# Two matmuls on the same weights become one of 512 columns, and the halves are added on the way out

## The chip, the cores and the metric

One NeuronCore of a Trainium2 chip runs the whole program. The metric is the device time of one execution in microseconds (us), taken as the median of three runs. TensorE (PE) multiplies into PSUM, an accumulator of eight banks of 512 float32 columns on each of 128 partitions. VectorE (DVE) and ScalarE (ACT) read PSUM and write SBUF. GpSimd (POOL) and SyncE (SP, which issues the weight loads) play a small part here.

## The reference, cut to what matters

Two layers work on a stream `h` of 256 tokens by 1024, float32. Each layer is a half step of SwiGLU, a mixer, and a second half step of SwiGLU; a last norm follows.

```
h = h + 1/2 * SwiGLU_a(RMSNorm(h))        # (silu(x @ w_gate) * (x @ w_up)) @ w_down, D_FF = 2816
u = RMSNorm(h);  z = u @ W_in             # columns: latents of MLA, diff q k v, pooling input p, gates
m = sum_i sigmoid(z_gate_i) * (y_i @ W_branch[i])
h = h + m @ W_out
h = h + 1/2 * SwiGLU_b(RMSNorm(h))
```

## The kernel before, in words

Every float32 operand of a product is split into two parts of 12 bits, `hi` and `lo`, so that three products of parts stand for one exact one: hi·hi, hi·lo and lo·hi. `mm3` (L162 to L165) issues these three matmuls into the same PSUM columns. Each matmul instruction is preceded by a load of its stationary operand, also when the operand is the same as before.

Two kinds of product exist. In `gemm_tokens` (L167) the stream is stationary and 512 (or 416) weight columns move. In `ffn` (gate and up products, L281 to L291) and in `gemm_dims` (L463 to L473; the columns C_P, C_DQ and C_DK of `W_in`) the weights are stationary: for each tile of 128 weight columns and each of the 8 tiles `k` of the contraction, `mm3` moves the 256 tokens of `u.xh(k)` and `u.xl(k)`. That is 4 half steps x 11 chunks x 2 weights x 2 tiles x 8 = 1408 calls in `ffn`, and 2 layers x 3 x 4 tiles x 8 = 192 in `gemm_dims`, 1600 triplets of 256 columns in all.

PSUM is used through three pools: four banks `acc`, three banks `tr` and one bank `o`. A chunk of `ffn` is 256 columns of gate and of up. In all chunks but the first, the two tiles of a weight share one bank, so a chunk takes two of the four `acc` banks. In the first chunk each tile has a bank of its own, two `acc` and two `tr`, of which half is used. `times` (L299) multiplies PSUM by the tokens' factors `rb` on the way out: one DVE instruction of 512 columns for each weight (L304), or four of 256 in the first chunk (L302). Then come SiLU on ACT (L307), the product of gate and up (L309) and its split into `ghi` and `glo` (L258, L259). `gemm_dims` puts two tiles into each bank, two banks for a call, and `scaled` (L475) takes each tile out with one DVE instruction (L478).

Each weight tile is loaded by one DMA on SP's queue, cast by ACT (`hi`, L158) and subtracted by DVE (`lo`, L159). There are three buffers each for the raw tile, `hi` and `lo`. `Norm` (L191) makes the stream's two parts: `hi` and `lo` are two tiles of [128, 8, 256], written half by half.

In the mixer `gemm_tokens` first makes the latents (C_CQ), whose two `acc` banks stay in use while squares, factors and copies are worked out (L429 to L447). Then follow C_P, C_DQ, the products of the latents (`mla_w_uq`, `ukv`), the attention, C_DK and C_DV. The order of instructions on each engine is not the order of the source: a planner in the framework sets it when the kernel is built, by program order and by what is ready and free. Each engine then runs its own list in order.

Of the kernel before, what the change touches and what calls it, by code (L numbers as in the profile page):

```python
# [11 lines left out]
F32 = mybir.dt.float32  # L12
F32R = mybir.dt.float32r
# [19 lines left out]
# columns of w_in  # L33
C_CQ, C_DQ, C_DK, C_DV, C_P, C_G = 0, 416, 928, 1440, 1952, 2464

# columns of the packed small parameters, per layer
# [8 lines left out]
def plan():  # L45
    """Weight tiles in the order of their use: (array, layer, first row tile, row tiles, first column, columns)."""
# [39 lines left out]
def trunk(ctx, tc, x, xt, positions, wall, small, lamrow, fnorm, out):  # L86
# [51 lines left out]
    # the input's loads, which go between those of the first weights  # L138
# [27 lines left out]

    def gemm_tokens(specs, xh, xl, n, before=None, tail=1):  # L167
        """Products with tokens on the partitions: one bank for each half of the tokens.

        The first half of the tokens is done ahead of the second in the last tiles, tail of them."""  # L170
# [15 lines left out]
    def rsqrt_mean(dst, src, n):  # L186
        """dst = (src / n + eps) ** -0.5"""
        nc.vector.tensor_scalar(out=dst, in0=src, scalar1=1.0 / n, scalar2=EPS, op0=ALU.mult, op1=ALU.add)
        nc.gpsimd.tensor_tensor(out=dst, in0=dst, in1=mhalf[:, :dst.shape[1]], op=ALU.pow)

    class Norm:  # L191
        """The transposed, scaled stream in two parts, and each token's factor, half by half."""

        def __init__(self, l, at):
            self.l, self.at = l, at
            self.hi = big([P, KD, S], F32R, "uhi")
            self.lo = big([P, KD, S], F32R, "ulo")
            self.ss = sp.tile([P, 2, 2], F32, tag="ss", name="ss", bufs=2)

        def half(self, n):  # L200
            for j in range(2):
# [7 lines left out]
                for i in range(2):  # L209
# [3 lines left out]
                    nc.scalar.activation(out=self.hi[:, k, :], in_=src, func=AF.Identity, scale=g)  # L213
                    nc.vector.scalar_tensor_tensor(
                        out=self.lo[:, k, :], in0=src, scalar=g, in1=self.hi[:, k, :].bitcast(F32),
# [3 lines left out]
        def first(self, k):  # L219
            """A tile of the same from the input, which comes in both layouts."""  # L220
            g = col(self.l, self.at + k)
            nc.sync.dma_start(out=xT[:, k, :], in_=xt[k * P:(k + 1) * P])
            nc.vector.tensor_scalar(out=self.hi[:, k, :], in0=xT[:, k, :], scalar1=g, scalar2=None, op0=ALU.mult)
            nc.vector.scalar_tensor_tensor(out=self.lo[:, k, :], in0=xT[:, k, :], scalar=g,
                                           in1=self.hi[:, k, :].bitcast(F32), op0=ALU.mult, op1=ALU.subtract)
# [12 lines left out]
        def row(self):  # L238
            """The factors along the free dimension, on every partition."""
# [9 lines left out]
        def xh(self, k):  # L249
            return self.hi[:, k, :]  # L250

        def xl(self, k):
            return self.lo[:, k, :]

    def split_evac(hi, lo, src, scale=None):
        """PSUM or SBUF -> the two parts, times a constant or a column."""
# [8 lines left out]
    def ffn(l, pre, u, following, midway=None):  # L265
        ghi = [big([P, 8, S], F32R, "ghi") for _ in range(3)]
        glo = [big2([P, 8, S], F32R, "glo") for _ in range(3)]
        for c in range(0, DFF, S):
            if c == 1024 and midway:
                midway(g[:, 0, :2])  # L270
            # transposed products, weights stationary: two tiles of each
            opened = bool(opening)
            w = [wsplit((f"{pre}_w_{n}", l, 0, KD, c, S)) for n in ("gate", "up")]
            if c == 0:
                # a bank for each tile, so that the first half of the stream serves them all
                ps = [[b()[:, :S] for _ in range(2)] for b in (acc, trp)]
                halves = [range(0, 4), range(4, 8)]
                order = [(n, i, k) for ks in halves for n in range(2) for i in range(2) for k in ks]
                if opened:
                    order = [(n, i, k) for n in range(2) for k in range(KD) for i in range(2)]  # L280
            else:  # L281
                banks = [acc() for _ in range(2)]
                ps = [[b[:, i * S:(i + 1) * S] for i in range(2)] for b in banks]
                order = [(n, i, k) for n in range(2) for i in range(2) for k in range(KD)]
            for n, i, k in order:
                wh, wl = w[n]
                ms = slice(i * P, (i + 1) * P)
                mm3(ps[n][i], wh[:, k, ms], wl[:, k, ms], u.xh(k), u.xl(k), k == 0, k == KD - 1)
# [10 lines left out]
            def times(dst, n):  # L299
                if c == 0:  # L300
                    for i in range(2):
                        nc.vector.tensor_tensor(out=dst[:, i, :], in0=ps[n][i], in1=rb, op=ALU.mult)  # L302
                else:
                    nc.vector.tensor_tensor(out=dst, in0=banks[n].rearrange("p (i s) -> p i s", i=2), in1=rbb, op=ALU.mult)  # L304
# [31 lines left out]
    # groups of heads in one bank of scores, every other head, on the same rows: (query tile, heads, keys)  # L336
# [3 lines left out]
    def tables(after):  # L340
        pi = sp.tile([P, 2], I32, tag="pi", name="pi", bufs=1)
        pr = tp.tile([P, S], I32, tag="C", name="pr")
        # the loads wait until the stream is under way
# [4 lines left out]
        # distances, exact where float32 holds them  # L348
# [22 lines left out]
        # rotary angles, reduced to [-pi, pi]  # L371
# [23 lines left out]
        # the learned lambda of each layer, and the head norm's gain times 1 - lambda_init  # L395
# [13 lines left out]
    def rope(eng, dst1, dst2, x1, x2, cos, sin, shape, out_shape=None):  # L409
        """The rotation of [x1 | x2]."""  # L410
# [9 lines left out]
    def mixing(l, u, following):  # L420
        wi = lambda c, n: [("w_in", l, k, 4, c, n) for k in (0, 4)]
        # -- latents and the shared rotary key
# [33 lines left out]
        # -- pooling input and differential q, k, transposed; v  # L456
# [6 lines left out]
        def gemm_dims(c, evac):  # L463
            w = [wsplit(spec) for spec in wi(c, 512)]
            for j in range(2):
                ps = acc()
                for i in range(2):
                    m = j * 2 + i
                    for k in range(KD):
                        wh, wl = w[k // 4]  # L470
# [379 lines left out]
```

## Time and profile before

| what | value |
|---|---|
| median of three runs (lowest, highest) | 1235.31 us (1235.24, 1237.77) |
| span of the profiled execution, first to last instruction | 1231.7 us |
| time outside that span, against the median | 3.6 us |
| mean granted clock of TensorE, of full speed | 0.999 |
| HBM traffic over the span | 172 GB/s |

The profile is of one execution. Its page gives the span and not that execution's own time from end to end. Busy times overlap (a matmul's record contains its run through the array), so the distance from one start to the next, not the recorded duration, is what a matmul costs in a stream.

### The profile page before, as it was taken

How to read it: one execution, taken by the hardware profiler on the slowest of the kernel's cores; microseconds unless marked ns; L12 is line 12 of the kernel's file. 1: busy time of each engine (PE TensorE's matmuls, PEld its weight loads, DVE VectorE, ACT ScalarE, POOL GpSimd, SP SyncE). 2: the span in 40 equal slices, each digit the busy share in tenths (PEclk: the TensorE clock that was granted, in tenths of full speed). 3: DMA queues.
4: the chain of work that ended last, by engine and by line, in shares of the span. 5: the costliest groups of instructions: out<-in, count | busy, mean ns of one | idle time of the engine just before them, and what ended most of it. 6: DMA issues, size and time to landing. Idle time of an engine off the chain costs nothing.

```text
span 1231.7 us, 19142 instructions
## 1 busy us (share of the span) xinstructions
PE 1216.1 (99%) x7912; PEld 1108.6 (90%) x7912; DVE 792.4 (64%) x1281; ACT 576.9 (47%) x891; POOL 69.3 (6%) x126
## 2 busy tenths in 40 slices
PE   7999999999999999999999999999999999999997
PEld 7999989998788899998899998899978888999986
DVE  6776655777757666664576664568686485766653
ACT  5454444446544554443454443455455444544442
POOL 0000000700100000000000000024010000000000
PEclk9999999999999999999999999999999999999999
DMA  8655455325345545554555555544343554455551
GB/s 276 239 184 181 175 181 191 120 93 189 137 171 176 192 172 179 181 191 168 187 199 176 191 182 188 175 146 145 110 165 135 177 202 171 171 188 188 189 171 68
DMA packets 34631, 213.13 MB, mean 173 GB/s; under 512 B 4080, under 2 KB 5488, under 8 KB 10992
## 3 DMA queue, kind: packets, MB, share of 16 engines
q1 hardware_dynamic: 33408, 210.52, 48.3%
q10 hardware_dynamic: 1136, 1.40, 0.4%
q8 instruction: 62, 1.02, 0.3%
q14 instruction: 25, 0.20, 0.1%
HBM read 210.85 MB, written 1.05 MB: 172 GB/s over the span
## 4 chain that ended last, share of the span: by engine, by line
PE 94%; DVE 3%; issue 2%; ACT 0%; DMA 0%; SPq 0%; POOLq 0%; POOL 0%
PE acc L163 28%; PE acc L164 28%; PE acc L165 28%; PE o L589 2%; PE tr L555 2%; PE tr L582 1%; PE tr L546 1%; PE tr L206 1%; DVE lo L159 1%; PE tr L163 1%; PE tr L165 1%; PE tr L164 1%; DMA xT<-xt 0%; PE tr L602 0%; PE acc L658 0%
## 5 line engine op out<-in xcount | busy, mean ns | idle before, releaser
L158 ACT CAST hi<-raw 128x1024 fp32r<-128x1024 f32 (+2 forms) x416 | 403.6, 1005 | 512.4 <-issue 326.3
L159 DVE TENSOR_TENSOR lo<-raw,hi 128x1024 fp32r<-128x1024 f32 (+2 forms) x416 | 481.4, 1173 | 223.1 <-ACT hi L158 222.2
L163 PE MATMUL acc<-uhi,hi 128*128 128x256 f32 x1536 | 439.2, 286 | 5.6 <-ACT hi L158 5.6
L165 PE MATMUL acc<-uhi,lo 128*128 128x256 f32 x1536 | 437.7, 285 | 1.5 <-DVE lo L159 1.5
L164 PE MATMUL acc<-ulo,hi 128*128 128x256 f32 x1536 | 437.7, 285 | 0.0
L163 PEld LDWEIGHTS acc<-uhi,hi 128*128 128x128 f32 x1536 | 296.7, 193 | 5.8 <-ACT hi L158 5.6
L165 PEld LDWEIGHTS acc<-uhi,lo 128*128 128x128 f32 x1536 | 296.6, 193 | 2.3 <-DVE lo L159 2.1
L164 PEld LDWEIGHTS acc<-ulo,hi 128*128 128x128 f32 x1536 | 296.8, 193 | 0.3
L164 PE MATMUL acc<-lo,ghi 128*128 128x512 f32 x352 | 137.4, 390 | 0.0
L165 PE MATMUL acc<-hi,glo 128*128 128x512 f32 x352 | 137.3, 390 | 0.0
L163 PE MATMUL acc<-hi,ghi 128*128 128x512 f32 x352 | 137.2, 390 | 0.0
L164 PE MATMUL acc<-lo,uhi 128*128 128x512 f32 (+1 forms) x256 | 99.6, 389 | 0.0
L163 PE MATMUL acc<-hi,uhi 128*128 128x512 f32 (+1 forms) x256 | 99.4, 390 | 0.0
L165 PE MATMUL acc<-hi,ulo 128*128 128x512 f32 (+1 forms) x256 | 98.8, 386 | 0.0
L163 PEld LDWEIGHTS acc<-hi,ghi 128*128 128x128 f32 x352 | 66.1, 188 | 13.5
L165 PEld LDWEIGHTS acc<-hi,glo 128*128 128x128 f32 x352 | 66.1, 188 | 13.5
L164 PEld LDWEIGHTS acc<-lo,ghi 128*128 128x128 f32 x352 | 66.1, 188 | 13.5
L304 DVE TENSOR_TENSOR g<-acc,rb 128x512 f32<-128x512 f32 x40 | 27.7, 693 | 78.5 <-PE acc L165 78.5
L574 ACT ACTIVATE e<-e,mx 128x128 f32<-128x128 f32 (+1 forms) x96 | 42.8, 446 | 57.4 <-DVE mx L570 35.4
L304 DVE TENSOR_TENSOR sg<-acc,rb 128x512 f32<-128x512 f32 x40 | 27.7, 692 | 49.6 <-PE acc L165 49.6
L164 PEld LDWEIGHTS acc<-lo,uhi 128*128 128x128 f32 x256 | 48.1, 188 | 9.7 <-issue 1.3
L163 PEld LDWEIGHTS acc<-hi,uhi 128*128 128x128 f32 x256 | 48.0, 188 | 9.3 <-issue 0.7
(199 smaller groups left out, 1222.4 us busy)
## 6 DMA issues: line engine op xcount, KB each, us to landing
raw<-wall SPq DMA_DIRECT2D x184, 1024.0 KB, 4.8
raw<-wall SPq DMA_DIRECT2D x10, 512.0 KB, 3.5
raw<-wall SPq DMA_DIRECT2D x18, 256.0 KB, 5.4
raw<-wall SPq DMA_DIRECT2D x4, 832.0 KB, 4.4
raw<-wall SPq DMA_DIRECT2D x2, 768.0 KB, 4.1
xT<-xt SPq DMA_DIRECT2D x8, 128.0 KB, 4.6
h<-x SPq DMA_DIRECT2D x4, 256.0 KB, 5.8
fn<-fnorm ACTq DMA_DIRECT2D x1, 512.0 KB, 3.8
```

Source lines behind the costliest of these rows:

```text
L158: nc.scalar.copy(out=hif[:, ks], in_=rawf[:, ks])
L159: nc.vector.tensor_tensor(out=lof[:, ks], in0=rawf[:, ks], in1=hif[:, ks].bitcast(F32), op=ALU.subtract)
L163: nc.tensor.matmul(ps, lhsT=lh, rhs=rh, start=start, stop=False)
L164: nc.tensor.matmul(ps, lhsT=lh, rhs=rl, start=False, stop=False)
L165: nc.tensor.matmul(ps, lhsT=ll, rhs=rh, start=False, stop=stop)
L206: nc.tensor.transpose(out=ps[:, (i * 2 + t) * P:(i * 2 + t + 1) * P], in_=h[:, t, k * P:(k + 1) * P], identity=ident)
L304: nc.vector.tensor_tensor(out=dst, in0=banks[n].rearrange("p (i s) -> p i s", i=2), in1=rbb, op=ALU.mult)
L546: nc.tensor.matmul(ps[:, i * nk:(i + 1) * nk], lhsT=qT[:, hd, qt * P:(qt + 1) * P], rhs=kT[:, hd, :nk], start=True, stop=True)
L555: nc.tensor.matmul(ps[:, i * nk:(i + 1) * nk], lhsT=dqT[a:a + 32, hd // 2, qt * P:(qt + 1) * P], rhs=dkT[a:a + 32, hd // 2, :nk], start=Tr ...
L574: nc.scalar.activation(out=e[:, sl], in_=e[:, sl], func=AF.Exp, bias=mx[:, i:i + 1], scale=-(2.0 ** -(hd + 1)) if slope else -1.0, accum_o ...
L582: nc.tensor.transpose(out=ptr[:, j * P:(j + 1) * P], in_=e[:, j * P:(j + 1) * P], identity=ident)
L589: nc.tensor.matmul(o[:, hd * 64:(hd + 1) * 64], lhsT=eT[:, j * P:(j + 1) * P], rhs=v[:, kt, hd * 64:(hd + 1) * 64], start=(kt == 0), stop= ...
```

## The change

A new `mm_wide` replaces `mm3` where weights are stationary. The stream's two parts lie side by side in new tiles `u` of [128, 4, 2, 256], one for each half of the contraction. A first matmul with `wh` moves both parts, 512 columns, into a whole bank; a second with `wl` moves the 256 columns of `xh` onto the bank's first half. `joined` puts the halves together: ACT copies the second half to SBUF, and DVE adds the first half to it. Each tile of 128 weight columns now has a bank of its own: a chunk of `ffn` takes four `acc` banks (two `acc` and two `tr` in the first chunk, as before), and a call of `gemm_dims` four. The multiplication by `rb` follows from SBUF, 512 columns at a time, or by the former instruction of `scaled`. In `gemm_dims` the intermediate sum lies in a buffer `both` of tag C, of which there are two. `gemm_tokens` is as before. The rest of the diff takes comments away.

```diff
+    def mm_wide(ps, wh, wl, u, k):
+        nc.tensor.matmul(ps, lhsT=wh, rhs=u.both(k), start=k == 0, stop=False)
+        nc.tensor.matmul(ps[:, :S], lhsT=wl, rhs=u.xh(k), start=False, stop=k == KD - 1)
+    def joined(dst, ps):
+        nc.scalar.copy(out=dst, in_=ps[:, S:])
+        nc.vector.tensor_tensor(out=dst, in0=ps[:, :S], in1=dst, op=ALU.add)
...
-            self.hi = big([P, KD, S], F32R, "uhi")
-            self.lo = big([P, KD, S], F32R, "ulo")
+            self.u = [big([P, 4, 2, S], F32R, "u") for _ in range(2)]
...
-            return self.hi[:, k, :]
+            return self.u[k // 4][:, k % 4, 0, :]
...
-            return self.lo[:, k, :]
+            return self.u[k // 4][:, k % 4, 1, :]
+        def both(self, k):
+            return self.u[k // 4][:, k % 4].rearrange("p e s -> p (e s)")
...
-            if c == 0:
-                ps = [[b()[:, :S] for _ in range(2)] for b in (acc, trp)]
...
-            else:
-                banks = [acc() for _ in range(2)]
-                ps = [[b[:, i * S:(i + 1) * S] for i in range(2)] for b in banks]
+            ps = [[b() for _ in range(2)] for b in (acc, trp if c == 0 else acc)]
...
-                mm3(ps[n][i], wh[:, k, ms], wl[:, k, ms], u.xh(k), u.xl(k), k == 0, k == KD - 1)
+                mm_wide(ps[n][i], wh[:, k, ms], wl[:, k, ms], u, k)
...
-                if c == 0:
-                    for i in range(2):
-                        nc.vector.tensor_tensor(out=dst[:, i, :], in0=ps[n][i], in1=rb, op=ALU.mult)
-                else:
-                    nc.vector.tensor_tensor(out=dst, in0=banks[n].rearrange("p (i s) -> p i s", i=2), in1=rbb, op=ALU.mult)
+                for i in range(2):
+                    joined(dst[:, i, :], ps[n][i])
+                nc.vector.tensor_tensor(out=dst, in0=dst, in1=rbb, op=ALU.mult)
...
-            for j in range(2):
+            for m in range(4):
                 ps = acc()
-                for i in range(2):
-                    m = j * 2 + i
-                    for k in range(KD):
-                        wh, wl = w[k // 4]
-                        mm3(ps[:, i * S:(i + 1) * S], wh[:, k % 4, m * P:(m + 1) * P], wl[:, k % 4, m * P:(m + 1) * P],
-                            u.xh(k), u.xl(k), k == 0, k == KD - 1)
-                evac(j, ps.rearrange("p (i s) -> p i s", i=2))
+                for k in range(KD):
+                    wh, wl = w[k // 4]
+                    mm_wide(ps, wh[:, k % 4, m * P:(m + 1) * P], wl[:, k % 4, m * P:(m + 1) * P], u, k)
+                evac(m, ps)
...
-            def evac(j, ps):
-                for i in range(2):
-                    nc.vector.scalar_tensor_tensor(out=dst[:, j * 2 + i, :], in0=ps[:, i, :], scalar=const_(j * 2 + i), in1=rb,
-                                                   op0=ALU.mult, op1=ALU.mult)
+            def evac(m, ps):
+                both = tp.tile([P, S], F32, tag="C", name="both")
+                joined(both, ps)
+                nc.vector.scalar_tensor_tensor(out=dst[:, m, :], in0=both, scalar=const_(m), in1=rb,
+                                               op0=ALU.mult, op1=ALU.mult)
```

## Rows read from the trace of the kernel before

**Rows 1.** The page's first part: busy time of an engine, share of the span, instructions. PE and DVE.

```profile
PE 1216.1 (99%) x7912; PEld 1108.6 (90%) x7912; DVE 792.4 (64%) x1281; ACT 576.9 (47%) x891; POOL 69.3 (6%) x126
```

**Rows 2.** The waits of PE over the whole span: what waited for what, us in total, times, longest in us. These are all of them.

```profile
PE acc L163 <- ACT hi L158: 5.6, 1, 5.6
PE acc L165 <- DVE lo L159: 1.5, 2, 1.0
PE acc L163 <- DVE k L527: 1.0, 2, 0.5
PE o L589 <- DVE eT L584: 0.5, 2, 0.2
PE acc L163 <- DVE qr L518: 0.2, 1, 0.2
```

**Rows 3.** Instructions of one form, grouped by line (count | busy us, mean ns of one | idle before). The first product of a triplet with weights stationary, in `acc` and in `tr` banks.

```profile
L163 PE MATMUL acc<-uhi,hi 128*128 128x256 f32 x1536 | 439.2, 286 | 5.6 <-ACT hi L158 5.6
...
L163 PE MATMUL tr<-uhi,hi 128*128 128x256 f32 x64 | 18.4, 287 | 0.0
```

**Rows 4.** The timeline of PE: start us, duration us, line, operation. First and last of stretches without a gap: 25 matmuls of 256 columns in a chunk (24 distances), 19 of 512 columns in the down product (18 distances), 27 of 416 columns (26 distances), 12 of 256 columns on weights of 64 columns (11 distances).

```profile
80.11 0.28 PE L165 MATMUL acc<-uhi,lo 128*128 128x256 f32 x1
...
82.99 0.28 PE L165 MATMUL acc<-uhi,lo 128*128 128x256 f32 x1
...
149.81 0.39 PE L163 MATMUL acc<-hi,ghi 128*128 128x512 f32 x1
...
153.89 0.39 PE L163 MATMUL acc<-hi,ghi 128*128 128x512 f32 x1
...
204.82 0.36 PE L163 MATMUL acc<-hi,uhi 128*128 128x416 f32 x1
...
209.71 0.35 PE L165 MATMUL acc<-hi,ulo 128*128 128x416 f32 x1
...
238.42 0.27 PE L163 MATMUL acc<-cTh,hi 128*64 128x256 f32 x1
...
239.67 0.28 PE L165 MATMUL acc<-cTh,lo 128*64 128x256 f32 x1
```

**Rows 5.** The same view in the opening: 21 matmuls of 256 columns (20 distances), before the distances fall to those of rows 4 at 16.7 us.

```profile
12.06 0.42 PE L164 MATMUL acc<-ulo,hi 128*128 128x256 f32 x1
...
16.33 0.40 PE L163 MATMUL acc<-uhi,hi 128*128 128x256 f32 x1
```

**Rows 6.** Instructions of one form on DVE and ACT, whole span (count | busy us, mean ns of one | idle before): a DVE product of a PSUM operand and an SBUF operand at 256 and at 512 columns, a DVE product of two SBUF operands at 512, and an ACT instruction from PSUM at 256.

```profile
L302 DVE TENSOR_TENSOR sg<-acc,rb 128x256 f32<-128x256 f32 x8 | 3.0, 416 | 0.0
...
L304 DVE TENSOR_TENSOR sg<-acc,rb 128x512 f32<-128x512 f32 x40 | 27.7, 692 | 49.6 <-PE acc L165 49.6
...
L309 DVE TENSOR_TENSOR g<-g,sg 128x512 f32<-128x512 f32 x44 | 30.4, 692 | 1.9 <-ACT sg L307 0.5
...
L517 ACT ACTIVATE qn<-acc 128x256 f32<-128x256 f32 x8 | 2.9, 384 | 2.4 <-PE acc L165 2.3
```

**Rows 7.** The timeline of DVE in two chunks of the first half step: start us, duration us, instruction, and in brackets the idle time before it and who ended it. All the idle stretches of one period are here; the last row is the first one a chunk later.

```profile
87.27 0.69 DVE L304 TENSOR_TENSOR sg<-acc,rb 128x512 f32<-128x512 f32 x1 [1.46 <-PE acc L165]
88.27 1.23 DVE L159 TENSOR_TENSOR lo<-raw,hi 128x1024 fp32r<-128x1024 f32 x1 [0.31 <-ACT hi L158]
89.74 1.23 DVE L159 TENSOR_TENSOR lo<-raw,hi 128x1024 fp32r<-128x1024 f32 x1 [0.25 <-ACT hi L158]
93.03 0.69 DVE L304 TENSOR_TENSOR g<-acc,rb 128x512 f32<-128x512 f32 x1 [2.06 <-PE acc L165]
...
98.79 0.69 DVE L304 TENSOR_TENSOR sg<-acc,rb 128x512 f32<-128x512 f32 x1 [1.46 <-PE acc L165]
```

**Rows 8.** Timelines of PE and DVE in the mixers of layer 0 (near 210 us) and layer 1 (near 820 us): the first matmul of C_P, and the last instruction that reads the first bank of the latents.

```profile
210.14 0.47 PE L163 MATMUL acc<-uhi,hi 128*128 128x256 f32 x1
...
216.64 0.24 DVE L447 TENSOR_SCALAR kr<-acc,r 128x32 f32<-128x32 f32 x1
...
817.77 0.47 PE L163 MATMUL acc<-uhi,hi 128*128 128x256 f32 x1
...
823.97 0.24 DVE L447 TENSOR_SCALAR kr<-acc,r 128x32 f32<-128x32 f32 x1
```

**Rows 9.** The timeline of DVE after C_DQ in layer 0: the two instructions that empty C_DQ's second bank, and the next instruction with idle time before it. No idle time lies between. Below it one row of the busy times by stretch: start and end, length, then PE, PEld, DVE, ACT, POOL, the granted clock, DMA share, GB/s.

```profile
234.82 0.86 DVE L478 SCALAR_TENSOR_TENSOR d<-acc,sm,rb 128x256 f32<-128x256 f32 x2
...
254.37 0.42 DVE L567 CUSTOM_DVE_ANT_0 e<-tr,mask 128x256 f32<-128x256 f32 x1 [0.45 <-PE tr L546]
...
240.00:260.00 20.00, 19.43 (x150) 18.15 (x151) 18.26 (x56) 10.83 (x30) 0.00 (x0) 1.00 0.29 97
```

**Rows 10.** Timelines of PE and DVE in the opening: the first matmul of the second chunk, the last piece of `lo` for that chunk's gate weights, and the last piece for its up weights.

```profile
23.53 0.47 PE L163 MATMUL acc<-uhi,hi 128*128 128x256 f32 x1
...
24.26 0.68 DVE L159 TENSOR_TENSOR lo<-raw,hi 128x512 fp32r<-128x512 f32 x1
...
29.20 0.68 DVE L159 TENSOR_TENSOR lo<-raw,hi 128x512 fp32r<-128x512 f32 x1
```

More of the change, by code (lines that the diff above doesn't have):

```diff
@@ L212, in half @@
                     src = ps[:, i * S:(i + 1) * S]
-                    nc.scalar.activation(out=self.hi[:, k, :], in_=src, func=AF.Identity, scale=g)
+                    nc.scalar.activation(out=self.xh(k), in_=src, func=AF.Identity, scale=g)
                     nc.vector.scalar_tensor_tensor(
-                        out=self.lo[:, k, :], in0=src, scalar=g, in1=self.hi[:, k, :].bitcast(F32),
+                        out=self.xl(k), in0=src, scalar=g, in1=self.xh(k).bitcast(F32),
                         op0=ALU.mult, op1=ALU.subtract)
@@ L222, in first @@
             nc.sync.dma_start(out=xT[:, k, :], in_=xt[k * P:(k + 1) * P])
-            nc.vector.tensor_scalar(out=self.hi[:, k, :], in0=xT[:, k, :], scalar1=g, scalar2=None, op0=ALU.mult)
-            nc.vector.scalar_tensor_tensor(out=self.lo[:, k, :], in0=xT[:, k, :], scalar=g,
-                                           in1=self.hi[:, k, :].bitcast(F32), op0=ALU.mult, op1=ALU.subtract)
+            nc.vector.tensor_scalar(out=self.xh(k), in0=xT[:, k, :], scalar1=g, scalar2=None, op0=ALU.mult)
+            nc.vector.scalar_tensor_tensor(out=self.xl(k), in0=xT[:, k, :], scalar=g,
+                                           in1=self.xh(k).bitcast(F32), op0=ALU.mult, op1=ALU.subtract)
         def squares(self, n):
@@ L273, in ffn @@
             w = [wsplit((f"{pre}_w_{n}", l, 0, KD, c, S)) for n in ("gate", "up")]
-            if c == 0:
-                ps = [[b()[:, :S] for _ in range(2)] for b in (acc, trp)]
[L277 to L280, printed above, removed]
-            else:
-                banks = [acc() for _ in range(2)]
-                ps = [[b[:, i * S:(i + 1) * S] for i in range(2)] for b in banks]
+            ps = [[b() for _ in range(2)] for b in (acc, trp if c == 0 else acc)]
+            if c == 0 and not opened:
+                order = [(n, i, k) for ks in (range(0, 4), range(4, 8)) for n in range(2) for i in range(2) for k in ks]
+            elif c == 0:
+                order = [(n, i, k) for n in range(2) for k in range(KD) for i in range(2)]
+            else:
                 order = [(n, i, k) for n in range(2) for i in range(2) for k in range(KD)]
```

## The prediction

> **What bounds the kernel now.** I read the busy shares first: PE 99%, DVE 64%, ACT 47% [rows 1]. A busy PE proves little, because matmul records overlap, so the waits of PE come second: over the whole span they add up to 8.8 us, and 7.1 of those fall in the first 11 us, while the first weights arrive [rows 2]. After that PE lacks nothing for more than half a microsecond at a time. The kernel is bound by the number of PE slots and the length of each; weight loads, casts and evacuations fit behind. So the third view is the timeline of PE, for the distance between starts.
>
> In a chunk, 24 distances of 256 columns take 2.88 us, 120 ns each. 18 distances of 512 columns take 4.08 us, 226.7 ns. A line through both has 0.4167 ns a column (2.4 GHz) and 13.3 ns beside the columns. The third width lies on it: 26 distances of 416 columns take 4.89 us, 188 ns, where the line says 186.7. On weights of 64 columns the same 256 moving columns cost 113.6 ns (1.25 us for 11), so about half of the fixed part goes with the width of the weights: it belongs to the weight load that each matmul brings along [rows 4].
>
> **The change on PE.** A triplet now has three slots of 256 columns: 3 x 120 = 360 ns. After it, one of 512 and one of 256: 226.7 + 120 = 346.7 ns. The columns are the same 768; one fixed part goes, 13.3 ns. The trace has 1536 triplets in `acc` and 64 in `tr` [rows 3], so 1600 x 13.3 = 21.3 us. In the opening, 20 distances take 4.27 us, 213.5 ns each, which is 256 columns at 1.2 GHz with no visible fixed part [rows 5]; some 13 triplets run there and gain nothing, 0.2 us. PE's gain is 21.1 us, of which 18.6 in the gate and up products and 2.5 in `gemm_dims`. No row shows a 512 slot and a 256 slot in turn. The bounds are 13.3 ns a triplet (each keeps its measured distance) and nothing (a 512 slot that in turn costs two of 256, 240 ns). I take the first: the load for the next slot has at worst 120 ns to hide in, as it has in every triplet of before.
>
> A rule of the Trainium skill speaks against this sum. Rows 4 show 13.3 ns beside the columns. The page "TensorE: Matmul & The Clock Gate", section "Back-to-back issue gap", states N / 2.4 + 2.5 ns for a warm matmul; by that the change would give back only 1600 x 2.5 = 4.0 us. The three widths measured here decide for 13.3.
>
> **The change on ACT and DVE.** Each of the 200 groups of 8 triplets gains one ACT copy and one DVE add of 256 columns. By the nearest rows the copy costs 384 ns (ACT from PSUM, 256 columns) and the add 416 ns (DVE, one operand in PSUM, 256 columns). The product with `rb` costs 692 ns from SBUF as from PSUM, so moving it is free [rows 6]. In the first chunk four products of 256 become four adds and two products of 512. No DMA is added or moved, and POOL gets nothing.
>
> In a chunk of `ffn` DVE gains 4 x 0.42 = 1.7 us and ACT 1.5 us. DVE's idle time in a period of 11.52 us is 1.46 + 0.31 + 0.25 + 2.06 = 4.1 us [rows 7]. The period shrinks by 32 x 13.3 ns = 0.43 us, and 4.1 - 1.7 - 0.4 = 2.0 us stay free. The new wait is for banks: a chunk takes all four, so the next chunk's first matmul needs the first bank copied and added. That bank is full a quarter into the chunk, 2.8 us, and is wanted again at 11.1 us. Queued behind a copy that waits for PE are ACT's casts, and behind the add DVE's subtractions for weights two tiles on. The trace shows the planner taking a half chunk out as soon as it is full (DVE's 1.46 us idle at 87 us ends on PE, in the middle of the chunk [rows 7]), so I cost this at nothing. What hides it is 8.3 us of other banks' work; if the cover were gone, the first bank would take 0.38 + 0.42 = 0.8 us after the chunk's end (second rival).
>
> **Where the gain is given back.** (a) C_P. Before, two of the four `acc` banks hold the latents while C_P fills the other two for 11.5 us. Now C_P's third tile wants a third bank 16 x 346.7 ns = 5.5 us after its start, at 215.9 us in layer 0 and 823.5 in layer 1 with the slower first matmul. The latents' first bank is last read until 216.9 and 824.2 [rows 8]. PE waits 1.0 and 0.7 us, and up to 0.7 more in each if the first tile's add and scaling (416 and some 400 ns) come ahead of the latents' chain in DVE's queue. Together 1.7 to 3.1; I take 2.4.
>
> (b) After C_DQ. From 234.8 to 254.4 us DVE has no idle time [rows 9], and PE's only waits in mid-span end there (1.0 us on the keys' copy, both layers [rows 2]). The last tile adds 0.4 us to DVE here, but one of the two scalings that lay here goes ahead. The copy may stand behind casts on ACT. From 0 to 2 us a layer; I take 0.5, 1.0 in all.
>
> (c) C_DK fills PE's gaps in the attention, where DVE is at 18.3 of 20 us [rows 9]. It gains 1.7 us there, and `both` shares its two buffers with the attention's transposed weights. If other products can fill PE, it costs nothing; if not, 1.7 us or a little more a layer. I take 0.7, 1.4 in all.
>
> (d) The opening. The second chunk starts at 23.53 us, and DVE finishes `lo` of its gate weights at 24.94 and of its up weights at 29.88 [rows 10]. At 347 ns a triplet the last up piece is wanted at 23.5 + 22 x 0.347 = 31.1. The first chunk's extra product (some 1.2 us) and one add can push it to 31.4: 0.3 us, between 0 and 1.5. I take 0.4.
>
> The sum is 21.1 - 2.4 - 1.0 - 1.4 - 0.4 = 15.9 us. The profiled span goes from 1231.7 to 1215.8 us. The 3.6 us that lie between that span and the median stay: 1235.3 - 15.9 = 1219.4 us. With no costs it is 1214.2; with all at their upper bounds (3.1 + 4.0 + 3.4 + 1.5 = 12.0), 1226.2.
>
> **Rivals.** First, small stalls spread over the chunks. With 2 us free, DVE's queue may sometimes stand behind a copy that waits for PE, so that weights arrive late, above all near 65 us where the tables are made. At 0.2 us in each of 44 chunks 9 us more go: 1228. For it speaks that DVE's queue gets four waits for PE in a chunk in place of two; against it that weights are made up to a chunk ahead.
>
> Second, slower: banks run out at each chunk's end. It needs the planner to put the first bank's copy and add behind the chunk's last matmul, where the source has them. Then PE waits 0.8 us in each of some 40 chunks, 32 us, and with the forecast's gain the time is 1219.4 + 32 = 1251. It decides from 32 x 13.3 ns = 0.43 us a chunk, where it eats PE's gain. The mid-chunk evacuation in rows 7 speaks against it; that all four banks are now taken speaks for it.
>
> Third, the slots in turn give little: a 512 slot followed by a 256 slot keeps most of the third fixed part. At 4 us of gain and 5.2 us of costs the time is 1236.5; at no gain, 1240.5. The Trainium skill's 2.5 ns would put it at the first of these. The three widths of rows 4 speak against it.
>
> **How the numbers follow.** The forecast, 1214 to 1226, gets 0.70. The first rival, 1226 to 1232, gets 0.13. The third gets 0.08: 0.06 of it within 0.2% of before (2.5 us, about what a measurement of this kernel can tell from no change) and 0.02 above. The second gets 0.09. So faster is 0.83, same 0.06, slower 0.11. The range reaches from 1213, just under the case without costs, to 1231, which leaves out the slower cases, no change, and the end of the first rival.
>
> **What would show it.** In the changed trace a pair should start 346 to 347 ns after the pair before it, in a chunk of about 11.1 us. PE's waits should grow by some 5 us in the mixers and the opening, with the latents' bank first among them; chunks of `ffn` should show none. DVE should gain some 80 us of busy time (200 x 0.42, and little else) and ACT some 77. The prediction is wrong if the pair takes 355 ns or more, or if PE waits for an evacuation at the start of each chunk.

## The result, and the profile after

The changed kernel takes 1223.87 us (median of four runs, 1221.7 to 1224.24) where the kernel before takes 1235.28 (1231.12 to 1237.77, measured beside it): a ratio of 0.9912, with a 95% interval from 0.9886 to 0.9937. It is faster by 0.9%, or 11.4 us of the 15.9 forecast. The profiled execution took 1221.7 us with a span of 1219.9 and a mean granted clock of 0.996.

The page's first part, which answers to [rows 1]:

```profile
PE 1198.4 (98%) x6312; PEld 1020.0 (84%) x6312; DVE 856.3 (70%) x1473; ACT 637.4 (52%) x1091; POOL 73.8 (6%) x126
```

There are 1600 matmuls fewer. DVE gained 63.9 us and ACT 60.5, with 192 and 200 instructions more. The new rows by form, beside [rows 3] and [rows 6] (count | busy us, mean ns of one | idle before):

```profile
L169 PE MATMUL acc<-u,hi 128*128 128x512 f32 x1536 | 540.4, 395 | 5.9 <-ACT hi L158 5.4 <-DVE sg L175 0.5
L170 PE MATMUL acc<-u,lo 128*128 128x256 f32 x1536 | 432.3, 282 | 2.1 <-DVE lo L159 2.1
...
L175 DVE TENSOR_TENSOR sg<-acc,sg 128x256 f32<-128x256 f32 x88 | 36.6, 416 | 7.6 <-ACT sg L174 7.5
...
L174 ACT COPY sg<-acc 128x256 f32<-128x256 f32 x88 | 32.4, 369 | 35.9 <-PE acc L170 34.2 <-DVE g L175 1.6
```

The add costs the 416 ns forecast, the copy 369 where 384 were taken. The timeline of PE in a chunk, beside [rows 4]:

```profile
80.21 0.39 PE L169 MATMUL acc<-u,hi 128*128 128x512 f32 x1
...
82.98 0.39 PE L169 MATMUL acc<-u,hi 128*128 128x512 f32 x1
```

From 80.21 to 82.98 us lie 8 pairs: 346 ns each, as forecast. The waits of PE over the whole span, beside [rows 2]:

```profile
PE acc L169 <- ACT hi L158: 5.4, 1, 5.4
PE acc L163 <- DVE qr L524: 3.5, 4, 1.5
PE acc L170 <- DVE lo L159: 2.1, 2, 1.9
PE tr L608 <- DVE o L616: 1.6, 2, 0.8
PE o L595 <- DVE eT L590: 1.4, 6, 0.3
PE acc L163 <- DVE both L175: 0.5, 2, 0.3
PE acc L169 <- DVE sg L175: 0.5, 1, 0.5
```

The waits on `qr`, `o`, `eT` and `both` lie in the mixers. They sum to 7.0 us; in the kernel before, the mixers' waits (`k`, `eT` and `qr`) were 1.7 [rows 2]. All of PE's waits together go from 8.8 to 15.0 us. None comes in `ffn` beyond the first half step.

The times by stage come from the starts of landmark matmuls in PE's timeline: the last matmul, the first of the second chunk, the first transposition of a new `h`, of the latents (L494, 217.19 us in layer 0), of the merged branches, the first product of the pooling (L664, 280.05 us), and for C_P the product ahead of it that spreads the tokens' factors (L253, 205.66 us). All in us; the last column is what the shorter slots alone would change.

| stage | before | after | difference | by slots |
|---|---|---|---|---|
| start to the second chunk | 23.53 | 21.14 | -2.39 | see below |
| second chunk to the end of the first half step | 145.86 | 144.00 | -1.86 | -4.27 |
| C_P, layers 0 and 1 | 11.94, 11.95 | 11.53, 11.54 | -0.82 | -0.85 |
| latents' transposes to pooling, layer 0 | 60.70 | 62.86 | +2.16 | -0.85 |
| the same, layer 1 | 60.78 | 64.46 | +3.68 | -0.85 |
| pooling to merged branches, layers 0 and 1 | 110.95, 110.87 | 110.88, 112.52 | +1.58 | 0 |
| the three other half steps | 169.18, 189.07, 198.41 | 164.46, 184.36, 193.71 | -14.13 | -14.08 |

They add up to -11.78; the stages between, not listed, differ by 0.03 at most, and the last matmul starts at 1213.06 in place of 1224.80 us. The 2.39 us at the start are luck of the execution: the kernel before, profiled twice more, reached its second chunk at 20.49 and 21.35 us. In the first profile its matmuls of 256 columns kept their distance of 213 ns until 16.5 us [rows 5], in these two until 10.7 and 12.7; that this is 1.2 GHz follows from the distance alone, since the granted clock of the view reads 1.00 there.

### The profile page after: what moved, and what is told of

Its sections match the earlier page's. It is cut to its first block, busy times and chain, and to the rows that moved or that the text cites. A ratio compares the mean times of both kernels' runs of the same rounds, so it can differ in the third digit from the quotient of the medians.

```text
span 1219.9 us, 16352 instructions
## 1 busy us (share of the span) xinstructions
PE 1198.4 (98%) x6312; PEld 1020.0 (84%) x6312; DVE 856.3 (70%) x1473; ACT 637.4 (52%) x1091; POOL 73.8 (6%) x126
## 4 chain that ended last, share of the span: by engine, by line
PE 94%; DVE 4%; ACT 1%; DMA 1%; issue 1%; SPq 0%; POOLq 0%; POOL 0%; ACTq 0%; DVEq 0%
PE acc L169 28%; PE acc L170 15%; PE acc L163 14%; PE acc L165 14%; PE acc L164 14%; PE o L595 2%; PE tr L561 1%; PE tr L169 1%; PE tr L588 1%; DVE lo L159 1%; PE tr L552 1%; PE tr L215 1%; PE tr L170 1%; ACT hi L158 1%; DMA xT<-xt 0%
## 5 line engine op out<-in xcount | busy, mean ns | idle before, releaser
L169 PE MATMUL acc<-u,hi 128*128 128x512 f32 x1536 | 540.4, 395 | 5.9 <-ACT hi L158 5.4
L170 PE MATMUL acc<-u,lo 128*128 128x256 f32 x1536 | 432.3, 282 | 2.1 <-DVE lo L159 2.1
L169 PEld LDWEIGHTS acc<-u,hi 128*128 128x128 f32 x1536 | 288.2, 188 | 68.9 <-ACT hi L158 5.3
L170 PEld LDWEIGHTS acc<-u,lo 128*128 128x128 f32 x1536 | 291.1, 190 | 4.1 <-DVE lo L159 3.2
L163 PE MATMUL acc<-hi,u 128*128 128x512 f32 (+1 forms) x256 | 100.7, 393 | 0.5 <-DVE both L175 0.5
L165 PE MATMUL acc<-hi,u 128*128 128x512 f32 (+1 forms) x256 | 100.8, 394 | 0.0
L164 PE MATMUL acc<-lo,u 128*128 128x512 f32 (+1 forms) x256 | 100.5, 393 | 0.0
L165 PEld LDWEIGHTS acc<-hi,glo 128*128 128x128 f32 x352 | 66.1, 188 | 13.4
L165 PEld LDWEIGHTS acc<-hi,u 128*128 128x128 f32 x256 | 48.9, 191 | 10.3 <-issue 1.3
L163 PEld LDWEIGHTS acc<-hi,u 128*128 128x128 f32 x256 | 48.9, 191 | 9.9 <-DVE both L175 1.0
L164 PEld LDWEIGHTS acc<-lo,u 128*128 128x128 f32 x256 | 48.8, 191 | 9.4 <-issue 0.7
L174 ACT COPY sg<-acc 128x256 f32<-128x256 f32 x88 | 32.4, 369 | 35.9 <-PE acc L170 34.2
L272 DVE TENSOR_TENSOR glo<-g,ghi 128x512 fp32r<-128x512 f32 x44 | 30.4, 691 | 25.6 <-ACT ghi L271 25.6
```

Source lines behind the costliest of these rows:

```text
L163: nc.tensor.matmul(ps, lhsT=lh, rhs=rh, start=start, stop=False)
L164: nc.tensor.matmul(ps, lhsT=lh, rhs=rl, start=False, stop=False)
L165: nc.tensor.matmul(ps, lhsT=ll, rhs=rh, start=False, stop=stop)
L169: nc.tensor.matmul(ps, lhsT=wh, rhs=u.both(k), start=k == 0, stop=False)
L170: nc.tensor.matmul(ps[:, :S], lhsT=wl, rhs=u.xh(k), start=False, stop=k == KD - 1)
L174: nc.scalar.copy(out=dst, in_=ps[:, S:])
```

## The experiments

Each kernel computes the whole. Lines marked with + or - stand against the changed kernel, except where another is named.

### The change in ffn alone

`gemm_dims` and `scaled` as before, with three slots a triplet and two banks a call.

```diff
-            for m in range(4):
+            for j in range(2):
                 ps = acc()
...
-                    mm_wide(ps, wh[:, k % 4, m * P:(m + 1) * P], wl[:, k % 4, m * P:(m + 1) * P], u, k)
-                evac(m, ps)
+                        mm3(ps[:, i * S:(i + 1) * S], wh[:, k % 4, m * P:(m + 1) * P], wl[:, k % 4, m * P:(m + 1) * P],
+                            u.xh(k), u.xl(k), k == 0, k == KD - 1)
+                evac(j, ps.rearrange("p (i s) -> p i s", i=2))
```

> The wide matmul stays in the gate and up products; gemm_dims goes back to three matmuls of 256 columns, two tiles to a bank, emptied by one scaling each. Theory A (the change in ffn gives its full 18.4 us, and the change in gemm_dims takes some 4 to 7 us away in the mixers): 1235.3 - 18.4 = 1217 us, no wait of PE on the copy qr over 0.5 us, mean granted clock back at 0.999. Rival B (the mixers lose because PE now comes to them with another layout of the stream and another order, whatever gemm_dims does): PE's waits there stay at 1.5 us and the time at 1221 to 1224 us.

Measured: 1217.06 us (1215.61 to 1218.67), ratio 0.9855 [0.9832, 0.9877], against 1235.17 for the kernel before (19 runs, shared with the next three). Latents to pooling takes 60.81 and 60.80 us, within 0.11 of before the change. The waits of PE, without those of the opening:

```profile
PE acc L163 <- DVE k L535: 1.0, 2, 0.5
PE acc L169 <- DVE sg L175: 0.5, 1, 0.5
PE acc L163 <- DVE qr L526: 0.5, 2, 0.2
PE o L597 <- DVE eT L592: 0.5, 2, 0.2
```

The `o` and `both` waits are gone, and `qr` is down from 3.5 to 0.5. The change in `gemm_dims` costs more than it brings: the part that was left out here makes the kernel 6.8 us slower. Theory A holds in time and waits, but not for the clock: its granted mean is 0.996 in the profiled execution and 0.996 to 0.999 in all four.

### The change in gemm_dims alone

```diff
-                mm_wide(ps[n][i], wh[:, k, ms], wl[:, k, ms], u, k)
+                mm3(ps[n][i], wh[:, k, ms], wl[:, k, ms], u.xh(k), u.xl(k), k == 0, k == KD - 1)
```

and in `ffn` the former banks and `times`.

> The reverse: three matmuls of 256 columns in ffn as before the change, the wide matmul, the join and a bank for each tile in gemm_dims alone. Theory A: slower than before by 2 to 7 us, 1237 to 1242 us, with PE's wait of about 1.5 us for the copy qr in both layers. Rival B: gemm_dims alone gains its 2.5 us, about 1233 us.

Measured: 1237.51 us (1234.45 to 1239.0), ratio 1.0023 [1.0009, 1.0037]. C_P takes 11.52 us, latents to pooling 62.86 and 62.84, and PE's waits on `qr`, `o`, `eT` and `both` are those of the changed kernel to the tenth (3.5, 1.6, 1.4, 0.5). So the loss in the mixers belongs to this part alone, and with 62.84 us in layer 1 it comes without the further 1.6 that the changed kernel's profile has there.

### The new way out with the old slots

The 512-column matmul is split again; banks, copies and adds stay.

```diff
-        nc.tensor.matmul(ps, lhsT=wh, rhs=u.both(k), start=k == 0, stop=False)
+        nc.tensor.matmul(ps[:, :S], lhsT=wh, rhs=u.xh(k), start=k == 0, stop=False)
+        nc.tensor.matmul(ps[:, S:], lhsT=wh, rhs=u.xl(k), start=False, stop=False)
```

> As the changed kernel in layout, banks, copies and adds, but the 512-column matmul is issued as two of 256 columns on the same weights, into the two halves. If the gain is the third slot's fixed part: distances of 120 ns again, the gain of 21 us gone, 1223.9 + 21 = 1245 us, so slower than before by the cost of the new evacuation alone. Rival (the gain comes from how the banks are emptied, not from the slots): within 5 us of the changed kernel, 1219 to 1229 us.

Measured: 1236.91 us (ratio 1.0017 [1.0003, 1.0032]). The timeline of PE has 24 slots of 120 ns from 79.98 to 82.86 us:

```profile
79.98 0.28 PE L169 MATMUL acc<-u,hi 128*128 128x256 f32 x1
...
82.86 0.28 PE L169 MATMUL acc<-u,hi 128*128 128x256 f32 x1
```

The three later half steps take 169.16, 189.07 and 198.42 us, within 0.02 of the kernel before, with 132 copies and 132 adds in them (33 chunks of four). There the way out costs nothing. But the expected size was missed: with the copies and adds alone the kernel is 1.7 us slower, not some 10. The mixers lose only 1.1 us a layer (61.85), PE waits 2.9 us on `qr` and not at all on `o`. The loss in the mixers is not a price of the copies by themselves; it grows when PE's products beside them get shorter: the changed kernel's stage takes 1.0 us longer (62.86), with 0.85 us less of slots in it.

### A bank for each tile, without the copy and the add

`gemm_dims` with three slots of 256 columns and four banks a call, each taken out by one scaling from PSUM.

```diff
-                    mm_wide(ps, wh[:, k % 4, m * P:(m + 1) * P], wl[:, k % 4, m * P:(m + 1) * P], u, k)
+                    mm3(ps[:, :S], wh[:, k % 4, m * P:(m + 1) * P], wl[:, k % 4, m * P:(m + 1) * P],
+                        u.xh(k), u.xl(k), k == 0, k == KD - 1)
...
-                both = tp.tile([P, S], F32, tag="C", name="both")
-                joined(both, ps)
-                nc.vector.scalar_tensor_tensor(out=dst[:, m, :], in0=both, scalar=const_(m), in1=rb,
+                nc.vector.scalar_tensor_tensor(out=dst[:, m, :], in0=ps[:, :S], scalar=const_(m), in1=rb,
```

> Wide matmul in ffn; gemm_dims with three matmuls of 256 columns into one half of a bank of its own for each tile, emptied by one scaling from PSUM, no copy and no add. If the copies and adds of gemm_dims cost the time in the mixers: as the kernel with ffn alone, 1217 us. If the banks cost it (a bank for each tile, twice as many as before): PE waits for qr as in the changed kernel, 1221 to 1224 us.

Measured: 1217.31 us (1215.98 to 1219.56), ratio 0.9862 [0.9837, 0.9888]; latents to pooling 60.34 and 60.31. Four banks a call cost nothing, rather a little less than two. This kernel lacks the wide matmul in `gemm_dims` too; against the kernel with three slots, which has the same banks and slots there, the copy and the add cost 1.5 us a layer (61.85 for 60.34), and the shorter slots beside them the 1.0 more.

### C_DQ or C_DK, or both, as before

The former form of `gemm_dims` for one or both calls; C_P stays wide.

```diff
-        gemm_dims(C_DQ, scaled(dqT, lambda j: sm[:, SM_DS + j:SM_DS + j + 1]))
+        gemm_dims_n(C_DQ, lambda j: sm[:, SM_DS + j:SM_DS + j + 1], dqT)
...
-        gemm_dims(C_DK, scaled(dkT, lambda j: 1.0))
+        gemm_dims_n(C_DK, lambda j: 1.0, dkT)
```

C_DQ as before:

> As the changed kernel, but C_DQ alone goes back to three matmuls of 256 columns, two tiles to a bank, one scaling each. The stage from the latents' transpositions to the pooling products takes 60.7 us before and 62.9 in the changed kernel. If the copies and adds of C_DQ make DVE late for the copies qr: PE's wait for qr (1.7 us a layer) goes, and the stage takes about 61.6 us (62.9 + 0.4 for the slots - 1.7). If C_DK's in the attention cost it all: the wait for qr stays and the stage takes 63.3 us.

C_DK as before:

> As the changed kernel, but C_DK alone goes back to three matmuls of 256 columns and one scaling each. If C_DK's copies and adds cost the waits in the attention (for o, eT and both, 1.4 us a layer): these go, and the same stage takes about 61.9 us (62.9 + 0.4 - 1.4), with the wait for qr still there. If C_DQ costs it all: 63.3 us.

Both as before:

> Wide matmul and join in ffn and in C_P alone; C_DQ and C_DK as before the change. If C_P's part is free, as its stage in the changed kernel says (11.5 us for 11.9): the same stage at 60.7 to 60.9 us, C_P's at 11.5, and the time 0.8 us under that of the kernel with the wide matmul in ffn alone, 1216 us. If C_P's copies and adds cost something later: 1217 to 1219 us.

Measured, latents to pooling in layers 0 and 1: 61.43 and 61.41 us with C_DQ as before, 61.84 and 61.83 with C_DK as before, 61.30 and 61.35 with both, where the changed kernel has 62.86 in layer 0. The first two stages are near the 61.6 and 61.9 expected. The times are 1219.58 and 1216.95 us (one execution each) and 1218.6 (1216.79 to 1220.14, ratio 0.987 [0.9845, 0.9895]). The waits of PE with C_DQ as before:

```profile
PE acc L163 <- DVE k L547: 1.3, 2, 0.7
PE acc L163 <- DVE qr L538: 1.2, 2, 0.6
```

and with C_DK as before:

```profile
PE acc L163 <- DVE qr L538: 3.5, 4, 1.5
```

Each part has its own wait: `qr` falls from 3.5 to 1.2 us when C_DQ is undone, `both` goes when C_DK is, and `o` when either is. Over the stage with both undone, C_DQ alone adds 0.54 us, C_DK alone 0.13, the two together 1.56, which is more than the sum, although each takes 0.43 us of slots away. C_P alone saves 0.41 us in its own stage and gives 0.5 back in the next (61.30 for 60.81); the 1216 us first expected of the third kernel were missed, and the second figure given there held. It held in part by another cause: its first half step ran 1.2 us slower than the first experiment's, at the longer of the two steady distances of the last section.

### Less DVE time: the last product on GpSimd

The scale goes with the copy and the add, and GpSimd multiplies by `rb`.

```diff
-                joined(both, ps)
-                nc.vector.scalar_tensor_tensor(out=dst[:, m, :], in0=both, scalar=const_(m), in1=rb,
-                                               op0=ALU.mult, op1=ALU.mult)
+                nc.scalar.activation(out=both, in_=ps[:, S:], func=AF.Identity, scale=const_(m))
+                nc.vector.scalar_tensor_tensor(out=both, in0=ps[:, :S], scalar=const_(m), in1=both,
+                                               op0=ALU.mult, op1=ALU.add)
+                nc.gpsimd.tensor_tensor(out=dst[:, m, :], in0=both, in1=rb, op=ALU.mult)
```

> Wide everywhere; in gemm_dims ACT scales its half on the copy, DVE scales and adds in one instruction, and GpSimd makes the product with the tokens' factors, so that DVE has one instruction a tile, as before the change. If DVE's second instruction costs the time in the mixers: the stage from the latents' transpositions to the pooling products at 59.9 to 61 us, and the time at 1216 to 1218 us. If the longer chain or the busy GpSimd (17 to 22 us of 24 in C_P's and C_DQ's stretch) costs as much: 62 us or more, 1222 us or more.

Measured: 1239.47 us, ratio 1.0034 [1.0018, 1.0051]; latents to pooling 69.63 and 70.04. The waits of PE:

```profile
PE acc L163 <- DVE both L484: 12.5, 7, 4.8
```

and the timeline of ACT at the longest of them:

```profile
235.53 0.47 ACT L483 ACTIVATE both<-acc,sm 128x256 f32<-128x256 f32 x1 [5.61 <-POOL d L486]
```

The two buffers of tag C now come free only when GpSimd, which works through its own list, has read them: ACT's copy stood idle 5.61 us for that. The rival wins: the copy's buffers became the bound, and this kernel does not tell what DVE time alone would be worth. Part of its time is the clock's: PE does nothing from 232 to 236 us, and from 234 to 242 us its granted clock is 0.50.

### The kernel before, twice more

The runs of the kernel before lie in groups: of 19, some at 1231.1 to 1231.4 us with a granted clock of 0.999, others at 1232.4 to 1232.5 (0.997), 1235.0 to 1235.7 (0.994) and 1237.8 to 1238.0 (0.993). Two profiles of it should show where.

> The kernel before, unchanged, for a second profile. Its other executions go from 1231 to 1238 us, in step with the mean granted clock (0.999 to 0.993), and the profile read for the prediction had 0.999. If the clock falls where PE has gaps: a stretch near the attention of one or both layers shows a granted clock of about 0.5 for some 3 us, the stages outside the mixers agree with those of the first profile within 0.1 us, and the span is 2 to 6 us over 1229.5. If the slower executions come from elsewhere (weights late, the opening): the difference lies in the first stage or in ffn.

> The same kernel once more, in case the profile before this one had the full clock. The same expectations.

Measured: 1235.21 us (span 1233.4, clock 0.994) and 1231.16 (span 1229.4, clock 0.999). In the slower one pooling to merged branches takes 112.53 and 114.09 us; in the other 110.87 and 110.86. The windows of the slower one (start and end, length, busy time and count of PE, PEld, DVE, ACT, POOL, granted clock, DMA share, GB/s):

```profile
324.00:328.00 4.00, 4.00 (x23) 2.98 (x21) 2.78 (x7) 1.99 (x2) 0.00 (x0) 1.00 0.45 188
328.00:332.00 4.00, 4.00 (x12) 3.03 (x11) 2.61 (x11) 2.19 (x8) 0.00 (x0) 0.57 0.19 39
...
928.00:932.00 4.00, 4.00 (x12) 2.96 (x13) 2.43 (x11) 1.99 (x7) 0.00 (x0) 0.63 0.07 10
...
940.00:944.00 4.00, 4.00 (x14) 3.16 (x13) 2.65 (x9) 2.42 (x9) 0.00 (x0) 0.66 0.41 117
```

PE's timeline in the first of these:

```profile
328.65 0.63 PE L165 MATMUL acc<-hi,ulo 128*128 128x512 f32 x1
...
331.21 0.63 PE L165 MATMUL acc<-hi,ulo 128*128 128x512 f32 x1
...
332.14 0.39 PE L165 MATMUL acc<-hi,ulo 128*128 128x512 f32 x1
...
333.96 0.39 PE L164 MATMUL acc<-lo,uhi 128*128 128x512 f32 x1
```

Near 330, 930 and 942 us the granted clock falls towards the lower of its two levels (0.5 is 1.2 GHz). Six distances of 512 columns take 2.56 us from 328.65, 427 ns each; eight take 1.82 us from 332.14, 228 ns each. Ahead of the fall, from 324.49 to 328.16 us, PE ran transposes, scores on 32 rows and products of 64 columns. The other profile ran the same instructions from 325.31 us on and kept a granted clock of 1.00. 112.53 - 110.87 = 1.66 us for the one drop in layer 0 and 114.09 - 110.86 = 3.23 for the two in layer 1: some 1.6 us each. The expected place, level and length are borne out, and the half steps agree; the opening does not (20.49 us for 23.53). The expectation looked for PE's gaps as the cause; that is not borne out, since PE is busy for all 4.00 us of each window. A record outlasts the distance to the next (0.28 us for 120 ns), though, so short gaps would not show.

### The first chunk as before

The first experiment's kernel, with the very first chunk in three slots and multiplied by `rb` straight from PSUM.

```diff
+                if opened:
+                    mm3(ps[n][i][:, :S], wh[:, k, ms], wl[:, k, ms], u.xh(k), u.xl(k), k == 0, k == KD - 1)
+                else:
+                    mm_wide(ps[n][i], wh[:, k, ms], wl[:, k, ms], u, k)
...
+                if opened:
+                    for i in range(2):
+                        nc.vector.tensor_tensor(out=dst[:, i, :], in0=ps[n][i][:, :S], in1=rb, op=ALU.mult)
+                    return
```

> As the kernel with the wide matmul in ffn alone, but the very first chunk of the program goes back to three matmuls of 256 columns and four scalings from PSUM (no copies, adds or products from SBUF). From the first triplet of the second chunk to the first transposition of the stream takes 145.9 us before and 144.0 with the wide matmul, where 141.6 were due; the second chunk alone takes 12.9 us for 11.7. If DVE's extra work on the first chunk delays the weights of the second: the second chunk in 11.3 to 11.9 us, that stretch in 142.5 to 143.2, and the time 0.5 to 1 us under 1217.1. If the stretch stays at 144.0 us and the second chunk at 12.9: the loss there has another cause.

Measured: 1216.51 us (1215.95 to 1219.6), ratio 0.9866 [0.9844, 0.9887]; not to be told from the first experiment by its time, but it can be by its stages. Counted by instructions, the second chunk takes 11.28 us (due by slots: 11.70 - 0.43 = 11.27), the next two 11.10 and 11.09. In the changed kernel it takes 12.19 (a count of the timeline's rows, some of which stand for two matmuls, gives 12.90), and the next three 11.31, 11.30 and 11.31. So the first chunk's new form causes both, its slots and its way out together; the way out alone, with the old slots, makes the second chunk 0.2 us longer (11.88 for 11.69). The stretch from the second chunk to the end of the half step falls only from 144.00 to 143.47 us, short of the 142.5 to 143.2 expected: the two chunks beside the tables take 11.56 and 12.48, and there PE waits 0.3 and 1.0 us for banks (`g` and `sg`), where the changed kernel waits 0.5.

## Why the prediction was right, and where not

**PE's gain: right to the nanosecond, outside the first half step.** 1600 x 13.3 ns was the term, with 18.6 us of it in `ffn`. The three half steps that nothing disturbs fell by 4.72, 4.71 and 4.70 us, for 11 x 32 x 13.3 ns = 4.69. No row of before showed a 512 slot and a 256 slot in turn; the bound that was taken (each keeps its measured distance) holds. The Trainium skill's page "TensorE: Matmul & The Clock Gate", section "Back-to-back issue gap", gives 2.5 ns beside the columns for the gap of a single matmul. For this stream, in which each matmul brings a weight load, it is not borne out: a pair of 346 ns in place of 360 gives back 13 to 14 ns. That the fixed part belongs to the weight load, as the prediction has it, rests on the one row with 64 columns of weights; no run tests it.

**The way out in ffn: right, free.** The three-slot kernel has it in all half steps, and the later three are as before within 0.02 us. Of the first rival (small stalls over the chunks) only the place it named came true, near the tables:

```profile
69.99 0.37 DVE L389 TENSOR_SCALAR kk<-kk 128x32 f32<-128x32 f32 x1
70.28 0.41 DVE L175 TENSOR_TENSOR sg<-acc,sg 128x256 f32<-128x256 f32 x1
```

The add that frees the bank stands in DVE's list behind the tables' work, and PE waits 0.50 us. The second rival (0.8 us at the end of each chunk) did not come. DVE's busy times, summed over the groups of its view by lines, go from 842.6 to 924.5 us: 81.9 for the 80 forecast. The page's busy time shows 63.9, since it counts records that overlap once (in the rows of the opening below, an instruction of 0.68 us is followed by the next after 0.59).

**Step (a), C_P waits for the latents' bank: failed.** 2.4 us (1.7 to 3.1) were forecast; there is no wait, and C_P gives its 0.41 us a layer. Timelines of PE and of DVE after, near [rows 8]:

```profile
211.64 0.39 PE L169 MATMUL acc<-u,hi 128*128 128x512 f32 x1
```

```profile
209.91 0.42 DVE L175 TENSOR_TENSOR both<-acc,both 128x256 f32<-128x256 f32 x1
...
212.11 0.24 DVE L455 TENSOR_SCALAR kr<-acc,r 128x32 f32<-128x32 f32 x1
```

The third tile starts 16 pairs before the transposes, at 217.19 - 5.55 = 211.64 us. The latents' first bank is read until after 212.11. So the tile has taken another, and by the times it can only be C_P's own first one, whose copy and add are done at 210.3. The step assumed that the third tile takes the latents' bank, which would have cost 0.7 us here; it got one that was free.

**Steps (b) and (c), the mixers: right in place, too small.** 2.4 us were taken for both layers, with bounds at 7.4. Slots save 0.85 us between the latents' transposes and the pooling, and yet layer 0 takes 2.16 more: 3.0 us a layer, 6.0 in all. The first place is C_DQ's. PE's timeline, and DVE's ahead of it:

```profile
237.62 0.33 PE L163 MATMUL acc<-cTh,hi 128*64 128x256 f32 x1 [1.49 <-DVE qr L524]
```

```profile
231.52 0.42 DVE L175 TENSOR_TENSOR both<-acc,both 128x256 f32<-128x256 f32 x1
...
232.05 0.48 DVE L484 SCALAR_TENSOR_TENSOR d<-both,sm,rb 128x256 f32<-128x256 f32 x1
...
237.29 0.28 DVE L524 COPY qr<-acc 128x128 f32<-128x128 f32 x1
```

From 231.52 to 237.57 us DVE has no idle time. C_DQ's last add and scaling stand in it ahead of the ropes, the last `qr` copy stands behind them, and with it the bank that `ukv`'s next product needs. The prediction named this queue but took the keys' copy for PE's only wait in mid-span; that one is gone, and this larger one came, on the `qr` that already had 0.2 us in [rows 2]. The second place is C_DK's, in the attention (PE, then DVE):

```profile
268.11 0.66 PE L608 MATMUL tr<-ident,o 128*128 128x128 f32 x4 [0.78 <-DVE o L616]
269.04 0.50 PE L163 MATMUL acc<-hi,u 128*128 128x512 f32 x1 [0.27 <-DVE both L175]
```

```profile
267.37 0.69 DVE L616 TENSOR_TENSOR o<-o,rs 128x512 f32<-128x512 f32 x1
267.98 0.68 DVE L272 TENSOR_TENSOR y<-tr,y 128x512 fp32r<-128x512 f32 x1
268.57 0.74 DVE L175 TENSOR_TENSOR both<-acc,both 128x256 f32<-128x256 f32 x2
```

C_DK fills PE's gaps in the attention. It is shorter now and ends earlier; the next filler, C_DV, needs a bank that C_DK holds until DVE comes to its add, and PE stands still on both. The prediction's "if other products can fill PE, it costs nothing" was the right question with the wrong answer. That a bank a tile is not to blame, and that the two calls together cost more than each alone, the experiments show; that the three-slot kernel loses less because its filler lasts longer is argued from its missing `o` wait, not shown by a run.

**A clock loss that stood in no step.** In layer 1 the same stage takes 64.46 us, 1.6 more than in layer 0. Windows after:

```profile
866.00:868.00 2.00, 1.13 (x9) 0.99 (x9) 1.94 (x4) 2.00 (x5) 0.00 (x0) 1.00 0.00 0
868.00:870.00 2.00, 1.73 (x7) 1.30 (x8) 2.00 (x6) 1.71 (x4) 0.00 (x0) 0.74 0.59 225
870.00:872.00 2.00, 2.00 (x6) 1.58 (x5) 2.00 (x6) 0.26 (x1) 0.00 (x0) 0.50 0.71 299
872.00:874.00 2.00, 2.00 (x9) 1.64 (x8) 2.00 (x2) 0.00 (x0) 0.00 (x0) 0.91 0.00 0
```

PE is busy for 1.13 and 1.73 of 2 us, the granted clock falls to 0.5, and PE's next matmuls of 512 columns start 0.43 us apart in place of 0.23. The gaps alone do not decide it: in layer 0 PE is busy for 1.10 and 1.62 of 2 us at the same place, and the granted clock stays at 1.00; in the kernel with the change in `gemm_dims` alone, with the same waits, it stays in both layers. The 1.65 us after the pooling in layer 1 are a drop of the kind that the kernel before has too.

**Step (d), the opening: right in place, too small.** 0.4 us (0 to 1.5) were taken; 4.27 - 1.86 = 2.4 went. The second chunk takes 12.19 for 11.27 due (0.9), three chunks after it 0.21 each above 11.09 (0.6), the chunk of the tables 11.92 (0.8). The 0.6 is no wait but a longer distance between pairs (353 ns, last section), which stood in no step. DVE in the second chunk, near [rows 10], and the matmul that waits:

```profile
22.57 0.68 DVE L312 TENSOR_TENSOR sg<-sg,rb 128x512 f32<-128x512 f32 x1
23.16 0.68 DVE L312 TENSOR_TENSOR g<-g,rb 128x512 f32<-128x512 f32 x1
23.77 0.68 DVE L159 TENSOR_TENSOR lo<-raw,hi 128x512 fp32r<-128x512 f32 x1
...
26.27 0.39 PE L170 MATMUL acc<-u,lo 128*128 128x256 f32 x1 [0.23 <-DVE lo L159]
```

The chunk's `lo` pieces stand behind the first chunk's two products from SBUF. The step asked only when the last piece is due; the early ones are late.

**The sum.** Costs of 5.2 us were forecast. Found are 0 for (a), 6.0 for (b) and (c), 2.4 for (d): 8.4, and 21.1 - 8.4 = 12.7. The medians moved by 11.4; the 1.3 between are about the size of one clock drop, but which drops a median execution of the changed kernel has, no profile shows. That the time lies inside 1214 to 1226 is in part luck: (a), 2.4 too high, offsets some of the 5.6 by which (b) to (d) were too low. The prediction's "3.6 us between span and median" were really 1.8 outside the span, as in every profiled run here, and a net 1.8: a median execution loses some 4 us to lower clock (1235.3 for 1231.2), and the profiled one had lost some 2 in its slow opening (23.53 us for 21.35).

## What to carry to other kernels

When a kernel is bound by PE slots, two matmuls on the same weights into one bank save the fixed part of one slot, and the distances of three widths in the trace of before price it (13.3 ns, and 13.4 measured). Where DVE has idle time in each chunk, as in `ffn`, the added evacuation work is free; where DVE runs without idle time it costs more than the slots give (3.0 us a layer for 0.85), since what counts is which copy stands behind it and whose bank that copy frees. Keep such a change out of those stages: in `ffn` alone it gives 18.1 us (1217.06 for 1235.17), in all places 11.4.

## What the runs showed of the hardware

Pairs of a 512 slot and a 256 slot have two steady lengths. After the opening the changed kernel runs at the longer one, and changes at a wait (PE's timeline):

```profile
29.80 0.40 PE L169 MATMUL acc<-u,hi 128*128 128x512 f32 x1
...
35.80 0.40 PE L169 MATMUL acc<-u,hi 128*128 128x512 f32 x1
...
70.74 0.50 PE L169 MATMUL acc<-u,hi 128*128 128x512 f32 x1 [0.50 <-DVE sg L175]
```

17 pairs from 29.80 to 35.80 us are 353 ns each, at a granted clock of 1.00; behind the wait at 70.74 they are 346 to 347. With C_DQ as before, and with C_DQ and C_DK as before, the chunks of the first half step ran at 353 to its end (11.3 us each), and with the first chunk as before none of it. A wait alone does not set it: with C_DQ as before PE waits 0.7 us at the tables and stays at 353. What sets the one or the other is open. The granted clock fell to its lower level in a stretch of the differential attention where PE's records show no idle time, in some executions of the kernel before and not in others, for some 1.6 us each time. And the opening, up to the second chunk, took 20.49, 21.35 and 23.53 us in three executions of the same kernel.
